# Moving the casts of a job of seven products to its head, and three position tables to a later load

## The chip, the cores and the metric

The kernel runs on one core of one Trainium2 chip. The metric is the device time of one execution in microseconds (us); the time of a version is the median of its runs. The core's engines appear under the names of the profile: PE is TensorE (matmuls; PEld are its weight loads), DVE is VectorE, ACT is ScalarE, POOL is GpSimd, SP is SyncE, which here only issues DMAs. Each engine works through its own instructions in the order in which they were recorded, and waits for the others through semaphores.

## The reference

One layer of a hybrid decoder trunk on a sequence of 512 positions and 1024 features. What matters here is the wide projection of the normed input and what is made of its columns:

```python
u = rmsnorm(x, ln1_g[i])
proj = u @ w_in[i]
q, k, v, pool_in, z, xbc, dt_raw, gate_pre = jnp.split(proj, split_idx, axis=-1)
y_a = dilated_attention_mixer(q, k, v, rel_bias) @ w_a[i]
y_b = pool_mixer(pool_in, pool_w[i], pool_scale[i]) @ w_b[i]
y_c = ssd_mixer(z, xbc, dt_raw, ...) @ w_c[i]
gates = jax.nn.sigmoid(gate_pre + b_gate[i]).reshape(b, s, N_BRANCH, D_MODEL)
merged = gates[:, :, 0] * y_a + gates[:, :, 1] * y_b + gates[:, :, 2] * y_c
x = x + merged @ w_o[i]
x = x + conv_ffn(rmsnorm(x, ln2_g[i]), ...)
return rmsnorm(x, final_g)
```

The attention has three groups of six heads with dilations 1, 4 and 16. Its scores get a bias by relative position, `rel_bias[bucket]`, which differs from group to group.

## The kernel before

Precision. Every operand of a matmul is a pair of float32r tiles, a high part and the rest. `cast` (line 185) makes the high part of a weight, `wh`, on ScalarE, in two halves; `lows` (line 208) makes the rest, `wl`, on VectorE by subtraction; `mm3` (line 228) multiplies high by high, high by low and low by high, so that `wl` is needed only in the last third of a chain of matmuls. There are three `wh` buffers, two `wl` buffers and two `raw` buffers for weights as they come from memory.

Jobs. The program is a list of jobs, one for each block of weights. The loop at line 1708 records them one after the other. For job n, `prepare` (line 1715) records first, at the head of the job: the subtraction of weight n+1, the cast of weight n+2, and the load of weight n+3. Then comes the job's body: matmuls and evacuations. `cast` is called with `spread`: its two halves are not recorded at once but put into the list `second`, and each `step()` in the body (and the `flush` loop ahead of the next job) records one of them.

Seven products. The second gate (`gate_seven(1)`), the values of attention groups 1 and 2 (`v_pair`) and the queries and keys of group 1 (`qk_sevens(1)`) are each computed by seven products of half-size blocks in place of eight. `Seven` (line 344) makes their jobs, called here by the names in the code: two, five, three, one, six, seven, and four. Five, three, six and seven have no load of their own: their weights are sums and differences that VectorE makes in the tiles W[0] and W[1] (`total`, L359, called by `then` behind a subtraction). Four's weight is loaded as raw and gets W[0] added to it, also at L359, when its cast is recorded. The order in the program is

```
gate: two five three one six seven
values: two, (gate four), five three one six seven
queries and keys: two, (values' four), five three one six seven
xbc 0, (queries' four), xbc 1, ...
```

Body of such a job (line 363): two halves of matmuls into two PSUM banks, each followed by its evacuation, and a single `step()` at the end. Two, five and three copy their banks to tiles r on ScalarE (L379). One, six and seven add the bank to r on VectorE (for the gate L741, for the values L661, for queries and keys L725); for the gate, sigmoids on ScalarE follow (L747), and `total` of the gate (L735) multiplies the merged branch by them on VectorE. One, six, seven and four accumulate in the same two banks, so a job's first matmul there waits until the sum that reads the bank is done.

What sets the order on ScalarE. Because the only step is at the end of the body, both halves of the spread cast, from the `step()` and from the `flush` loop, stand behind the job's evacuations.

Position tables. `bias_rows` (line 526) computes the biases by position, writes them to a DRAM tile `rd`, and loads six tables from there (L561): b0 to b2 for group 0, b3 to b5 for group 1, whose right half later takes group 2 (`residues`, line 572). These tables, like most working tiles, come from the pool `big`, which has 52 slots under one tag; a new tile takes a slot and waits for the last readers of the tile that held it. `rows` runs while the values of group 0 are computed; the attention of group 1 starts after the first xbc job. SP issues all loads in the order of their recording, unless a scheduler changes places between neighbours.

Of the kernel before, what the change touches and what calls it, by code (L numbers as in the profile page):

```python
# [16 lines left out]
P = 128  # L17
# [54 lines left out]
class Job:  # L72


    def __init__(self, parts, k, c, body):
        self.parts, self.k, self.c, self.body = parts, k, c, body
        self.raw = self.split = None
        self.late = self.short = False
        self.load = self.form = self.then = None


# [1 line left out]
def trunk(ctx: ExitStack, tc, out, x, rel_bias, ln1_g, w_in, b_gate, w_a, pool_w, pool_scale, w_b,  # L83
# [3 lines left out]
    act, dve, pool, pe, sp = nc.scalar, nc.vector, nc.gpsimd, nc.tensor, nc.sync  # L87
# [18 lines left out]
    def T(name, dt=F32, shape=(P, S)):  # L106
        return big.tile(list(shape), dt, name=name, tag="t")

    def MM(name):
        return psum.tile([P, S], F32, name=name, tag="mm")  # L110

    def SM(name):
        return psum.tile([P, S], F32, name=name, tag="sm")
# [230 lines left out]
    class Seven:  # L344


        def __init__(self, quarter, c, widths, product, done, name):
            R, A, B, W = {}, [], [], [None, None]

            def tile_of(i):  # L350
                W[i] = ypool.tile([P, 4, S], F32, name="w3", tag="xs")[:, :, :c]
                sp.dma_start(W[i], quarter(i, 1))

            def plus():
                for k in range(4):
                    pool.dma_start(W[0][:, k, :], quarter(0, 0)[:, k, :], accum_op=OP.add)

            def total(out, a, b, op=OP.add):
                dve.tensor_tensor(out, a, b, op)  # L359
                return out  # L360

            def job(j, raw, form, bank, use, more=False):
                def body(ws):
                    if not more:
                        bank[:] = [MM(name) for _ in range(2)]
                    for i in range(2):
                        product(bank[i], ws, side_u(j), i, more)
                        use(i, bank[i][:, :widths[i]])
                    step()
                new = Job([raw] if raw is not None else [], 4, c, body)  # L370
                new.form = form
                if raw is None:
                    new.load = lambda: None
                return new

            def keep(hi, right):
                def use(i, ps):
                    r = R[hi, right, i] = T("r7")[:, :widths[i]]
                    act.copy(r, ps)  # L379
                return use  # L380

            def end(hi, right, op=None):
                return lambda i, ps: done(hi, right, i, R.get((hi, right, i)), ps, op)

            self.two = job("A12", quarter(1, 0), None, B, keep(0, 0))
            five = job(1, None, lambda: W[0], B, keep(1, 1))
            three = job(4, None, lambda: W[1], B, keep(0, 1), True)
            one = job("A11", quarter(0, 0), None, A, end(0, 0, OP.add))
            six = job(2, None, lambda: W[0], A, end(0, 1, OP.subtract), True)
            seven = job(3, None, lambda: W[1], A, end(1, 1, OP.subtract), True)  # L390
            four = self.four = job("A22", quarter(1, 0), lambda: total(four.raw, four.raw, W[0]), A,
                                   end(1, 0), True)
            five.then = lambda: total(W[0], W[0], W[1])
            one.then = lambda: total(W[1], W[0], one.raw, OP.subtract)
            self.jobs = five, three, one, six, seven
            self.load = lambda: tile_of(0), plus, lambda: tile_of(1)
# [127 lines left out]
    bias = []  # L524

    def bias_rows():


        relb, hot = T("relb"), [T(f"hot{i}") for i in range(2)]

        hr, two = [T(f"hotr{i}", F32R) for i in range(2)], T("relp", F32R)
        rh, rl = two[:, :18], two[:, 18:36]
        dve.memset(relb[:, :18], 1.0)
        sp.dma_start(relb[:BUCKETS, :18], rel_bias)
        sp.dma_start(hot[0][:BUCKETS + 1, :S], c_hot[:, :S])
        sp.dma_start(hot[1][:BUCKETS + 1, :R_ALL - S], c_hot[:, S:])

        def part(tiles, lo, n):
            i = lo // S
            return tiles[i][:, lo - i * S:lo - i * S + n]  # L540

        def rows():
            rv = [T(f"rv{i}") for i in range(2)]
            rd = dram.tile([HEADS, R_ALL], F32, name="rdram")
            ps_r = [SM("psr0"), SM("psr1")]
            for g, (off, n) in enumerate(zip(R_OFF, R_LEN)):
                lo = off
                while lo < off + n:
                    m = min(off + n, (lo // S + 1) * S) - lo
                    for r in (rh, rl):  # L550
                        pe.matmul(part(ps_r, lo, m)[:HEADS], r[:BUCKETS + 1, 6 * g:6 * g + 6],
                                  part(hr, lo, m)[:BUCKETS + 1], start=r is rh, stop=r is rl)
                    lo += m
            for i in range(2):
                m = (S, R_ALL - S)[i]
                dve.tensor_copy(rv[i][:HEADS, :m], ps_r[i][:HEADS, :m])
                sp.dma_start(rd[:, i * S:i * S + m], rv[i][:HEADS, :m])
            for i in range(6):
                b = T(f"b{i}")
                g, width = (0, 256) if i < 3 else (1, P)  # L560
                sp.dma_start(b[:, :2 * width].rearrange("p (h c) -> p h c", h=2),  # L561
                             spans(rd, g, i % 3, P, width))
                bias.append(b)
            bias.append(rd)
            return
            yield

        def spans(rd, g, c, high, width):
            return bass.AP(tensor=rd.tensor, offset=rd.offset + R_OFF[g] + 2 * c * R_ALL,
                           ap=[[1, high], [R_ALL, 2], [1, width]])  # L570

        def residues():
            rd = bias.pop()
            for c in range(3):
                b = bias[3 + c][:, 256:]
                dve.memset(b, NEG)
                for a in range(0, P, 32):
                    sp.dma_start(b[a:a + 32].rearrange("p (h c) -> p h c", h=2)[:, :, a:a + 32],
                                 spans(rd, 2, c, 32, 32))
                yield  # L580

        def parts():
            n = BUCKETS + 1
            dve.tensor_copy(rh[:n], relb[:n, :18])
            dve.tensor_sub(rl[:n], relb[:n, :18], rh[:n].bitcast(F32))
            for i in range(2):
                m = (S, R_ALL - S)[i]
                dve.tensor_copy(hr[i][:n, :m], hot[i][:n, :m])

        return rows, parts, residues  # L590

    def bias_of(g, h):
        if g == 0:
# [890 lines left out]
    def program():  # L1484
# [11 lines left out]
        for i, job in enumerate(branch_jobs(1, w_b, YB, 8, more=range(7))):  # L1496
            if i == 1:
                yield Call(gates.load[0])
            if i == 2:
                yield Call(lambda: running.extend(after(2 * p - 4, sums_of_u(p)) for p in (2, 3)))  # L1500
                yield Call(gates.load[1])
                yield Call(gates.load[2])
            yield job
        last = None
        for group, next_ in zip(groups, groups[1:] + (None,)):
            yield group.two
# [52 lines left out]
    weights = [j for j in jobs if isinstance(j, Job)]  # L1559
# [33 lines left out]
        (b_gate[0].rearrange("(c p) -> c p", p=P), 24),  # L1593
        (pool_scale[0].rearrange("(c p) -> c p", p=P), 8)], "col")
    sp.dma_start(tri, c_tri)
    rows_of_bias, parts_of_bias, residues_of_bias = bias_rows()

    def row_squares(tb, ss, n=1, eng=dve):

# [67 lines left out]
    parts = lows(weights[1], 2)  # L1667
# [39 lines left out]
    n = 0  # L1707
    for job in jobs:
        if not isinstance(job, Job):
            job.fn()  # L1710
            continue
        while second:
            flush()
        if n >= 2:
            def prepare(n=n, later=False):

                def rest():
                    if n + 1 < len(weights):
                        low(weights[n + 1])
                    yield  # L1720
                    if n + 2 < len(weights):
                        cast(weights[n + 2], 2, spread=not later)
                    if n + 3 < len(weights):
                        fetch(weights[n + 3])
                if later:
                    return rest()
                for _ in rest():
                    pass

            if job.late:  # L1730
                job.prepare = prepare
            else:
                prepare()
            job.body(job.split)
        n += 1
# [40 lines left out]
```

## Time and profile before

| | |
|---|---|
| median of 3 runs | 1030.3 us (1029.78 to 1030.36) |
| the profiled execution, whole time | 1028.16 us |
| the profiled execution, its span | 1025.6 us |
| PE busy, share of the span | 1010.9 us, 99% |
| DVE busy | 707.7 us, 69% |
| ACT busy | 511.2 us, 50% |
| granted PE clock, mean | 0.998 |
| DMA, mean rate over the span | 119 GB/s |

Rows of the trace are read like this: a row of the timeline gives the start in us from the span's start, the duration, the engine, the line of the kernel, the operation, output<-input by the program's names, the shapes, how many instructions are merged in the row, and in brackets how long the engine was idle before and what ended that. A row of the chain of waits gives the start, the time that the chain spent there, the engine and the line. L12 is line 12 of the kernel; a line can be that of a helper, so that all casts are at L195 and nearly all matmuls at L236.

### The profile page before, as it was taken

What the parts mean: (1) busy time and instruction counts of PE and PEld (TensorE: products, weight loads), DVE (VectorE), ACT (ScalarE), POOL (GpSimd) and SP (SyncE); (2) the same over time, 40 slices, a digit from 0 to 9 for tenths busy, and PEclk for the clock granted to TensorE, in tenths of its full rate; (3) what the DMA queues carried; (4) which work ended last, traced back from release to release, by engine and by line L of the source; (5) the groups of instructions that cost most, each with busy time, mean ns of one, the idle gap of its engine ahead of it and who ended that gap; (6) DMA issues with size and microseconds to landing.
All of it is one profiled execution on the core that took longest, in us unless ns stands there. A gap on an engine that the chain in (4) does not pass through costs nothing.

```text
span 1025.6 us, 13613 instructions
## 1 busy us (share of the span) xinstructions
PE 1010.9 (99%) x5402; PEld 861.3 (84%) x5402; DVE 707.7 (69%) x886; ACT 511.2 (50%) x863; POOL 136.7 (13%) x120
## 2 busy tenths in 40 slices
PE   8999999989999999999999999999999999999997
PEld 8998877989988888888888888898888888888885
DVE  6554667568667655676889666767778768685756
ACT  5433545454536466788566234644444434433434
POOL 1781000010000000000043501102111100111002
PEclk9999999999999999999999999999999999999999
DMA  8548312044344445542254526532232232321322
GB/s 271 166 110 214 112 54 75 11 144 137 132 148 124 109 115 137 137 130 66 82 157 161 164 83 239 182 120 99 85 122 82 89 117 75 131 82 42 124 103 82
DMA packets 115629, 123.34 MB, mean 120 GB/s; under 512 B 6483, under 2 KB 96150, under 8 KB 115567
## 3 DMA queue, kind: packets, MB, share of 16 engines
q1 hardware_dynamic: 113247, 119.01, 37.3%
q0 software_dynamic: 1728, 2.62, 1.5%
q8 instruction: 42, 0.69, 0.3%
q10 hardware_dynamic: 592, 0.86, 0.3%
q14 instruction: 20, 0.16, 0.0%
HBM read 118.68 MB, written 3.00 MB: 119 GB/s over the span
## 4 chain that ended last, share of the span: by engine, by line
PE 95%; DVE 2%; ACT 2%; DMA 1%; issue 0%; ACTq 0%
PE pa L236 34%; PE pu L236 22%; PE pb L236 12%; PE pd L236 7%; PE pqk L236 6%; PE pq L236 3%; PE pa L1624 2%; PE ps L779 1%; PE pu L1414 1%; PE po L827 1%; PE ppw L236 1%; ACT wh L195 1%; DVE wl L215 1%; PE pt L813 1%; PE py L1112 1%; DMA xin<-in_x_dram 1%
## 5 line engine op out<-in xcount | busy, mean ns | idle before, releaser
L215 DVE TENSOR_TENSOR wl<-raw,wh 128x2048 fp32r<-128x2048 f32 (+3 forms) x92 | 214.1, 2328 | 60.6 <-ACT wh L195 52.7
L195 ACT CAST wh<-raw 128x1024 fp32r<-128x1024 f32 (+4 forms) x181 | 181.3, 1021 | 53.8 <-DVE raw L359 15.9
L1309 DVE SCALAR_TENSOR_TENSOR hc<-pu,fcol,hc 128x510 f32<-128x510 f32 x88 | 65.8, 748 | 56.5 <-ACT hc L1306 54.8
L236 PE MATMUL pa<-uh,wh 128*128 128x512 f32 (+1 forms) x368 | 88.9, 381 | 0.2 <-ACT wh L195 0.2
L236 PE MATMUL pa<-uh,wl 128*128 128x512 f32 (+1 forms) x368 | 86.9, 375 | 2.1 <-DVE wl L215 2.1
L236 PE MATMUL pa<-ul,wh 128*128 128x512 f32 (+1 forms) x368 | 86.8, 375 | 0.0
L236 PE MATMUL pu<-uh,wh 128*128 128x512 f32 (+1 forms) x352 | 83.5, 379 | 0.0
L236 PE MATMUL pu<-uh,wl 128*128 128x512 f32 (+1 forms) x352 | 83.5, 379 | 0.0
L236 PE MATMUL pu<-ul,wh 128*128 128x512 f32 (+1 forms) x352 | 83.5, 379 | 0.0
L236 PEld LDWEIGHTS pa<-uh,wl 128*128 128x128 f32 x368 | 66.7, 188 | 14.7 <-DVE wl L215 2.3
L236 PEld LDWEIGHTS pa<-ul,wh 128*128 128x128 f32 x368 | 66.7, 188 | 12.6
L236 PEld LDWEIGHTS pa<-uh,wh 128*128 128x128 f32 x368 | 65.3, 188 | 12.4 <-ACT wh L195 0.5
L236 PEld LDWEIGHTS pu<-uh,wl 128*128 128x128 f32 x352 | 64.2, 188 | 12.5
L236 PEld LDWEIGHTS pu<-ul,wh 128*128 128x128 f32 x352 | 64.2, 188 | 12.5
L236 PEld LDWEIGHTS pu<-uh,wh 128*128 128x128 f32 x352 | 64.1, 188 | 12.4
L1306 ACT ACTIVATE hc<-pu,fcol,fcol 128x512 f32<-128x512 f32 x40 | 31.2, 780 | 79.2 <-PE pu L236 79.2
L1314 POOL TENSOR_TENSOR hc<-hc 128x512 f32<-128x512 f32 x22 | 30.8, 1400 | 289.1 <-DVE hc L1309 244.4
L215 DVE TENSOR_TENSOR wl<-w,wh 128x2048 fp32r<-128x2048 f32 (+1 forms) x18 | 38.0, 2111 | 12.4 <-ACT wh L195 7.8
L801 ACT ACTIVATE sb<-sb,nmls 128x128 f32<-128x128 f32 (+1 forms) x72 | 30.0, 418 | 31.5 <-DVE nmls L798 21.4
L1095 POOL TENSOR_TENSOR st<-st,dts 128x512 f32<-128x512 f32 x4 | 4.2, 1053 | 228.9 <-ACT st L1103 166.8
L195 ACT CAST wh<-w 128x1024 fp32r<-128x1024 f32 (+1 forms) x36 | 32.8, 954 | 2.4 <-DVE w L341 2.4
L1311 ACT ACTIVATE hc<-hc 128x512 f32<-128x512 f32 x22 | 13.9, 632 | 39.9 <-DVE hc L1309 39.9
(409 smaller groups left out, 1923.1 us busy)
## 6 DMA issues: line engine op xcount, KB each, us to landing
raw<-in_w_in_dram SPq DMA_DIRECT2D x24, 1024.0 KB, 6.1
raw<-in_ffn_w_up_dram SPq DMA_DIRECT2D x22, 1024.0 KB, 5.2
raw<-in_w_o_dram SPq DMA_DIRECT2D x8, 1024.0 KB, 5.3
raw<-in_ffn_w_down_dram SPq DMA_DIRECT2D x8, 1024.0 KB, 5.1
raw<-in_w_in_dram SPq DMA_DIRECT2D x14, 512.0 KB, 4.8
raw<-in_w_in_dram SPq DMA_DIRECT2D x8, 768.0 KB
raw<-in_w_b_dram SPq DMA_DIRECT2D x4, 1024.0 KB, 5.2
w<-in_ffn_w_down_dram SPq DMA_DIRECT2D x4, 1024.0 KB, 5.0
```

Source lines behind the costliest of these rows:

```text
L195: (other.tensor_copy if other and i else act.copy)(job.high[:, :, o], job.raw[:, :, o])
L215: (eng or dve).tensor_tensor(l[:, :, o], job.raw[:, :, o], h[:, :, o].bitcast(F32), OP.subtract)
L236: pe.matmul(ps, l, r, start=first and n == 0, stop=last and n == total - 1, skip_group_check=onto)
L779: pe.matmul(pss[i][:, o:o + w * P], q[r, n * P:(n + 1) * P], k[r, kb * P:(kb + w) * P], start=True, stop=True)
L801: act.activation(sb[:, off:off + w * P], sb[:, off:off + w * P], AF.Exp, bias=nm[:, n, h:h + 1], accum_out=ls[:, n, h:h + 1])
L813: pe.transpose(pt[:, o:o + P], sb[:, o:o + P], eye)
L827: pe.matmul(po[DH * hh:DH * hh + DH, n * P:(n + 1) * P], V[g, kb + i][:, (2 * c + hh) * DH:(2 * c + hh + 1) * DH], probs[2 * c + hh, nb][: ...
L1306: act.activation(t, ps, AF.Identity, bias=ff["c1"][:, ff["b"] + m:ff["b"] + m + 1], scale=fw(2, m))
L1309: dve.scalar_tensor_tensor(t[:, sh:], ps[:, :S - sh], fw(k, m), t[:, sh:], OP.mult, OP.add)
L1311: act.activation(t, t, AF.Silu)
L1314: pool.tensor_tensor(a, a, t, OP.mult)
L1624: pe.matmul(first[2 * n + j][:, lo:hi], a[:, k, j * P:(j + 1) * P], b[:, k, lo:hi], start=a is wh and b is uh and k == 0, stop=a is wl and ...
```

## The change

Two things, both small in the text. Every job of seven products gets the mark `once`; while such a job is recorded, `prepare` calls `cast` without `spread`, so that both halves of the cast of weight n+2 are recorded at once, at the head of the job, ahead of its matmuls and evacuations. And the tables b3 to b5 are no longer loaded in `rows`, but by `second_table`, which `program` calls after the last `w_b` job and before the first job of the gate's group.

```diff
@@ class Job
-        self.late = self.short = False
+        self.late = self.short = self.once = False
@@ Seven.job
-                new.form = form
+                new.form, new.once = form, True
@@ bias_rows, rows
-            for i in range(6):
-                b = T(f"b{i}")
-                g, width = (0, 256) if i < 3 else (1, P)
-                sp.dma_start(b[:, :2 * width].rearrange("p (h c) -> p h c", h=2),
-                             spans(rd, g, i % 3, P, width))
-                bias.append(b)
+            table(rd, 0, 256)
             bias.append(rd)
             return
             yield
+
+        def table(rd, g, width):
+            for c in range(3):
+                b = T(f"b{c}")
+                sp.dma_start(b[:, :2 * width].rearrange("p (h c) -> p h c", h=2),
+                             spans(rd, g, c, P, width))
+                bias.append(b)
+
+        def second_table():
+            rd = bias.pop()
+            table(rd, 1, P)
+            bias.append(rd)
...
-        return rows, parts, residues
+        return rows, parts, second_table, residues
@@ program
             yield job
+        yield Call(lambda: second_table())
         last = None
@@ trunk
-    rows_of_bias, parts_of_bias, residues_of_bias = bias_rows()
+    rows_of_bias, parts_of_bias, second_table, residues_of_bias = bias_rows()
@@ the loop over jobs
-            def prepare(n=n, later=False):
+            def prepare(n=n, later=False, spread=not job.once):
...
-                        cast(weights[n + 2], 2, spread=not later)
+                        cast(weights[n + 2], 2, spread=spread and not later)
```

## The prediction

> **What bounds the kernel now.** I read the page's first two parts, then what TensorE waits for, then the stretches with waits. Columns of the page: engine, busy us, share of the span, instructions.
>
> ```profile
> span 1025.6 us, 13613 instructions
> PE 1010.9 (99%) x5402; PEld 861.3 (84%) x5402; DVE 707.7 (69%) x886; ACT 511.2 (50%) x863; POOL 136.7 (13%) x120
> ```
>
> TensorE bounds everything: no matmul is added or removed, so the change can win at most TensorE's idle time, 14.7 us, or add to it. Where is that idle time? The view of TensorE's waits, from 181 us to 310 (who waited for whom, us in total, times, longest):
>
> ```profile
> PE pa L236 <- DVE wl L215: 2.1, 1, 2.1
> PE pa L236 <- DVE r L741: 0.7, 1, 0.7
> PE pq L236 <- DVE q L725: 0.6, 1, 0.6
> ```
>
> These lie in the three groups of seven products, 181.69 to 284.60 us. Busy time there (stretch, length, PE, PEld, DVE, ACT, POOL, clock, DMA share, GB/s):
>
> ```profile
> 181.69:232.34 50.65, 47.68 (x395) 46.52 (x394) 32.15 (x24) 25.51 (x40) 3.53 (x4) 1.00 0.31 87
> 232.34:284.60 52.26, 51.47 (x362) 50.91 (x361) 39.10 (x34) 24.84 (x38) 0.00 (x0) 1.00 0.41 124
> ```
>
> TensorE is idle 2.97 us in the gate group and 0.79 us after it, at full clock, with ScalarE half busy: it is work in the wrong order, not too much work. The chain of waits (start, us, what) shows which order:
>
> ```profile
> 201.94 2.00 ACT wh L195 x2
> ...
> 207.93 0.91 ACT sg L747 x2
> 208.84 1.89 ACT wh L195 x2
> ...
> 210.76 2.29 DVE wl L215
> 213.05 0.61 DVE r L741
> ...
> 216.88 1.76 DVE wl L215
> 218.64 2.20 DVE raw L359
> 220.84 0.61 DVE r L741
> ...
> 222.29 0.90 ACT sg L747 x2
> 223.18 1.90 ACT wh L195 x2
> ...
> 225.10 2.30 DVE wl L215
> ...
> 227.45 5.05 PE pa L236 x40
> ...
> 262.25 8.64 PE pq L236 x72
> ...
> 274.46 1.16 DVE q L725 x2
> ```
>
> It is a ring. A cast (wh) of a later weight stands on ScalarE behind the sigmoids (sg) of the product that has just run; these wait for VectorE's sum (r); the sum stands behind the subtraction (wl) of the weight before; and that waits for its own cast. TensorE pays twice: it waits for a bank that a late sum still reads, and for a late wl.
>
> What it costs is best read from the starts of products:
>
> ```profile
> 207.12 0.71 PE L236 MATMUL pa<-sah,wh 128*128 128x256 f32 x4
> ...
> 213.79 0.71 PE L236 MATMUL pa<-sbh,wh 128*128 128x256 f32 x4 [0.69 <-DVE r L741]
> ...
> 219.62 0.86 PE L236 MATMUL pb<-wh,uh 128*128 128x384 f32 x4
> ...
> 224.17 0.74 PE L236 MATMUL pa<-uh,wh 128*128 128x256 f32 x4 [0.22 <-ACT wh L195]
> ...
> 232.34 0.86 PE L236 MATMUL pb<-wh,sah 128*128 128x384 f32 x4
> ...
> 236.51 0.85 PE L236 MATMUL pb<-wh,sbh 128*128 128x384 f32 x4
> ...
> 240.67 0.85 PE L236 MATMUL pb<-wh,uh 128*128 128x384 f32 x4
> ...
> 245.22 0.93 PE L236 MATMUL pb<-wh,sah 128*128 128x384 f32 x4 [0.22 <-ACT wh L195]
> ...
> 270.71 0.64 PE L236 MATMUL pq<-uh,wh 128*128 128x256 f32 x4
> ...
> 275.76 0.71 PE L236 MATMUL pq<-sah,wh 128*128 128x256 f32 x4 [0.57 <-DVE q L725]
> ```
>
> An unhindered product takes 5.83 us in the gate group (213.79 to 219.62), 4.17 with the values (232.34 to 236.51), 4.32 with queries and keys (half of 8.64, the chain's last row). Above that lie: gate six 0.84 (6.67 to seven's start), value two 0.38 (4.55), gate four 2.34 (8.17), value one 0.38 (4.55), query one 0.73 (5.05). Together 4.67 us.
>
> **The change, part one: casts at the head.** For a job of seven products, both halves of the cast of the weight two jobs on are put before its evacuations on ScalarE instead of behind them. Their count and size stay: two casts, 2.0 us for a gate weight. VectorE's and TensorE's orders are the same in both builds; only ScalarE's rows change places. I walk the queues by the durations above.
>
> Gate one (on TensorE up to 207.1): at 201.94 ScalarE now holds not six's cast, which already stands one evacuation earlier, but seven's. It ends near 203.9 instead of 210.73. Seven's subtraction (2.29) then waits only for its turn behind one's second sum (0.7 from 207.1), near 207.9, and ends at 210.2. Six's first half leaves TensorE at 207.12 + 2.9 = 210.0, its sum runs 210.2 to 210.9, and TensorE wants that bank at 212.9: 2 us of cover, and the 0.84 is gone.
>
> Gate four: after six's second sum (213.7), the subtraction for value two (1.76) ends at 215.5, and the sum for four (L359, 2.2) at 217.7. Four's cast now stands ahead of seven's sigmoids: 217.8 to 219.8, instead of from 223.18 on. Its subtraction, 2.30, ends at 222.1. TensorE reaches four at 212.9 + 5.8 + 4.2 = 222.9 and needs wl eight of its 48 matmuls later (1.0 us), at 223.9: 3.1 and 1.8 us of cover, so 0.38 and 2.34 are gone.
>
> What waits instead: ScalarE stands before four's cast from about 214.7 to 217.8, with seven's four sigmoids behind it. They end at 221.6, before 223.18 as now; only VectorE's gate multiplications read them. Nothing on TensorE does.
>
> The value and query groups go the same way: value six's subtraction waits no longer for a late cast but for value three to leave the wl buffer, at 228.7 + 2 x 4.17 = 237.0, and ends at 238.8; one's first sum follows as soon as TensorE gives it, near 239, and the 0.38 is gone. Query six: two sums of 1.16 us after one's first half end just as one's second half does, so of 0.73 I take 0.6 and leave 0.1. The heads whose cast waits for a sum on VectorE (value's and query's four) hold up only evacuations with over 2 us to spare.
>
> The casts' other two needs hold by the same walk. The wh buffer (three of them) is that of the job before, which TensorE has just left. The raw weight of gate four is asked for here:
>
> ```profile
> 202.77 0.39 SPq L182 DMA_DIRECT2D raw<-in_w_in_dram  x1
> raw<-in_w_in_dram SPq DMA_DIRECT2D x24, 1024.0 KB, 6.1
> ```
>
> It lands at 208.9 and is first read by the sum at 215.5. Part one: 0.84 + 0.38 + 2.34 + 0.38 + 0.6 = 4.5 us.
>
> [...] By busy time alone part one would be 2.97 + 0.79 = 3.8 us; by starts it is 4.5, and the starts carry the sum, since each wait also shows a drained pipe as busy.
>
> **Part two: three tables later.** The three 128 KB tables of groups 1 and 2 leave the queue of SP near 72 us and enter it behind value two's raw weight; in the changed build the latest thing they wait for is a matmul in the second half of the last job before the groups, near 180.
>
> ```profile
> 176.12 5.48 PE pa L236 x24
> ...
> 71.77 3.21 SPq L561 DMA_DIRECT2D b<-rdram  x6
> 180.00:190.00 10.00, 10.00 (x94) 9.34 (x93) 4.71 (x4) 3.69 (x7) 0.00 (x0) 1.00 0.00 0
> 308.53 0.68 DVE L794 SCALAR_TENSOR_TENSOR sb<-ps,b 128x512 f32<-128x512 f32 x1
> ```
>
> Six tables issue in 3.2 us, so three in 1.6; the DMA engines are idle from 180 to 190, and SP is free until 202.77. First use is at 308.53. Cost nothing, with over 20 us of cover in front of the weights.
>
> But the tables take no slots of the shared pool meanwhile, so every tile after them lands in another slot, and waits for other old readers. In the two builds' waits I find one that matters:
>
> ```profile
> 166.50 0.59 ACT L1018 ACTIVATE east<-pact 16x512 f32<-16x512 f32 x1 [3.23 <-PE po L827]
> ...
> 167.50 0.87 PE L827 MATMUL po<-sb,v 128*64 128x128 f32 x10 [0.82 <-ACT sb L814]
> ```
>
> Before, `east` stands in a slot that the po matmuls read: ScalarE waits 3.23 us, the copy of sb behind it is late, and TensorE waits 0.82 us. In the changed build `east` waits for no matmul. It can run at 163.3 (166.50 less 3.23), and the copy ends one us later, as now; TensorE asks for it at 166.7 (167.50 less 0.82), 2 us after. That is 0.8 us more. The other changed waits point at releases long past. Bounds: zero, if another wait takes its place, to 1.0 with the drain; I take 0.8, by the wait's own row.
>
> **Sum.** 4.5 + 0.8 = 5.3 us. After 284.60 TensorE waits for almost nothing until the tail, and loads are released by the same subtractions, so I let it reach the end. The profiled execution took 1028.16 us, 2.1 below the median of 1030.3; it would become 1022.9. Against the median: 1030.3 - 5.3 = 1025.0 us. About 2.1 us (0.2%) is what a measurement can tell from no change.
>
> **Rivals.** Gate four still waits (12%). If the serial run from 213.7 to 222.1 (subtraction, sum, cast, subtraction) is 4 us later than walked, the cover of 1.8 is used up and four keeps its 2.3: 5.3 - 2.3 = 3.0 us won, 1027.3. For it: this run is the longest on VectorE, and the cast now stands in its midst. Against: all its durations are measured ones.
>
> The change does not do what it says (8%). If a cast at the head cannot start before the old place, because wh or raw is not free, then only the slot's 0.8 is left, or later loads swallow the rest: 1029.5, within 0.2%. For it: three wh buffers only. Against: the walk above finds each free on time; the raw loads land with 6 us in hand.
>
> Slower (6%): the tables block SP. If their slots came free only when gate results do, near 232, four's raw weight behind them would be asked for at 232 instead of 202.77, land at 238, and TensorE would stand from 222.9 until cast and subtraction are through (238 + 2.2 + 2.0 + 2.3 = 244.5) less 1: some 20 us, 1030.3 - 5.3 + 20 = 1045. From 211 on (223.9 less 2.3, 2.0, 2.2 and 6.1) every us of delay costs one, and past 216 the change loses. The named releases, near 180, speak against it.
>
> **How the numbers follow.** Forecast 74%, its own range 1024.0 to 1026.5: busy time and slot alone give 3.8 + 0.8 = 4.6 (1025.7), all starts with the drain 4.67 + 1.0 = 5.7 (1024.6), and half a us for the median itself. To hold 8 in 10 I reach up into the first rival: 1023.7 to 1027.8. Faster 74 + 12 = 86%; same 8%; slower 6%.
>
> **What would show it.** In the changed profile: no wait of pa for wl or r, of pq for q, of po for sb; each gate product's start 5.8 us after the last; four's cast straight behind L359, sigmoids after it; value five near 228 on the old clock; the tables issued near 180. Any new wait of a matmul for wh, or for a raw load behind the tables, makes it wrong.

## The result, and the profile after

| | before | after |
|---|---|---|
| median of 6 runs each | 1030.03 us (1028.81 to 1030.36) | 1021.44 us (1021.24 to 1021.96) |
| the profiled execution, whole time | 1028.16 us | 1021.86 us |
| its span | 1025.6 us | 1019.9 us |

The ratio is 0.992, with a 95% interval of 0.9907 to 0.9933. The change gains 8.6 us by these medians, where the prediction had 5.3: the direction is right, the size too small, and the time lies below the predicted range. First what the profile shows of the steps.

The head of the page after, and then all that TensorE waits for in the whole span (who waited for whom, us in total, times, longest):

```profile
span 1019.9 us, 13619 instructions
...
PE 1010.3 (99%) x5402; PEld 862.2 (85%) x5402; DVE 707.4 (69%) x886; ACT 511.3 (50%) x863; POOL 136.4 (13%) x120
```

```profile
PE uT L1649 <- DVE diag L1661: 1.7, 2, 1.3
PE pa L1591 <- DVE ones L1582: 1.1, 1, 1.1
```

Busy times are those of before, engine by engine. The waits for wl, r and q in the groups of seven are gone, and so is the wait for sb at the po matmuls. What is left lies at the start of the kernel. TensorE's busy time moved by 0.6 us, the span by 5.7: nothing was made cheaper, TensorE only stands less.

The same two stretches as before (stretch, length, PE, PEld, DVE, ACT, POOL, clock, DMA share, GB/s):

```profile
181.69:232.34 50.65, 50.65 (x416) 50.32 (x415) 36.78 (x30) 29.32 (x47) 3.53 (x4) 1.00 0.36 100
232.34:284.60 52.26, 52.26 (x361) 51.09 (x360) 37.77 (x32) 22.09 (x34) 0.00 (x0) 1.00 0.43 134
```

TensorE now works through both without a gap, 416 matmuls in the first where there were 395.

The starts of the products, from the timeline of TensorE:

```profile
206.33 0.64 PE L236 MATMUL pa<-sah,wh 128*128 128x256 f32 x4
...
212.09 0.64 PE L236 MATMUL pa<-sbh,wh 128*128 128x256 f32 x4
...
217.85 0.86 PE L236 MATMUL pb<-wh,uh 128*128 128x384 f32 x4
...
222.01 0.64 PE L236 MATMUL pa<-uh,wh 128*128 128x256 f32 x4
...
227.76 0.86 PE L236 MATMUL pb<-wh,sah 128*128 128x384 f32 x4
...
236.09 0.85 PE L236 MATMUL pb<-wh,uh 128*128 128x384 f32 x4
...
240.25 0.85 PE L236 MATMUL pb<-wh,sah 128*128 128x384 f32 x4
...
265.67 0.64 PE L236 MATMUL pq<-uh,wh 128*128 128x256 f32 x4
...
270.06 0.71 PE L236 MATMUL pq<-sah,wh 128*128 128x256 f32 x4
...
278.90 2.00 PE L236 MATMUL pa<-uh,wh 128*128 128x512 f32 x8
```

Every gate product takes 5.75 or 5.76 us, every value product 4.16 or 4.17. Product by product against before:

| product | before | after | gained | predicted |
|---|---|---|---|---|
| gate six | 6.67 | 5.76 | 0.91 | 0.84 |
| value two | 4.55 | 4.16 | 0.39 | 0.38 |
| gate four | 8.17 | 5.75 | 2.42 | 2.34 |
| value one | 4.55 | 4.16 | 0.39 | 0.38 |
| query one | 5.05 | 4.39 | 0.66 | 0.6 |

From gate six's start to the first matmul behind the groups it took 284.60 - 207.12 = 77.5 us, and now takes 278.90 - 206.33 = 72.6: 4.9 us. Behind the groups nothing of it is lost again: 741.0 us are left to the end of the span in both.

The queue order that the walk predicted around gate four, on ScalarE and then on VectorE (start, us, engine, line, operation):

```profile
213.01 0.91 ACT L754 ACTIVATE sg<-r,col 128x256 f32<-128x256 f32 x2 [1.97 <-DVE r L748]
216.96 2.00 ACT L195 CAST wh<-raw 128x1024 fp32r<-128x1024 f32 x2 [3.04 <-DVE raw L359]
218.87 1.70 ACT L754 ACTIVATE sg<-r,col 128x256 f32<-128x256 f32 x4
```

```profile
214.56 2.29 DVE L359 TENSOR_TENSOR raw<-raw,w 128x2048 f32<-128x2048 f32 x1
...
218.99 2.29 DVE L215 TENSOR_TENSOR wl<-raw,wh 128x2048 fp32r<-128x2048 f32 x1 [0.25 <-ACT wh L195]
```

Four's cast waits 3.04 us for its sum, with seven's four sigmoids behind it, as walked; the subtraction ends at 221.28. TensorE reaches gate four at 222.01 and wants wl a us later: 1.7 us of cover, where the prediction had 1.8. The price that ScalarE pays, 3 us of standing, costs TensorE nothing.

The tables and `east` (the queue of SP; ScalarE):

```profile
177.61 1.77 SPq L566 DMA_DIRECT2D b<-rdram  x3
```

```profile
163.74 0.58 ACT L1025 ACTIVATE east<-pact 16x512 f32<-16x512 f32 x1
```

The three tables issue near 178 in 1.77 us; `east` waits for nothing. What that is worth is read from the chain of waits, before and after: a row at the start of the kernel, then the first row of the po matmuls and the next row of pa.

```profile
21.32 1.75 PE uT L1690 x16
...
165.45 1.07 PE po L827 x16
...
169.81 2.77 PE pa L236 x12
```

```profile
21.88 1.75 PE uT L1698 x16
...
166.00 1.68 PE po L834 x28
...
169.13 2.77 PE pa L236 x12
```

From po to pa it took 169.81 - 165.45 = 4.36 us and now takes 169.13 - 166.00 = 3.13: 1.23 us, where the prediction had 0.8 and at most 1.0. The first rows show something else: the profiled execution after was 0.56 us late by 21 us, ahead of both parts of the change. Over all the profiles of the experiments below, that row of uT starts between 21.1 and 22.2 us, and one of the late ones (21.86) belongs to a kernel with the tables at their old place; so the spans of single executions scatter by about a us, whatever the change does.

### The profile page after: what moved, and what is told of

It is laid out like the page before. It is cut to its first block, busy times and chain, and to the rows that moved or that the text cites. A ratio compares the mean times of both kernels' runs of the same rounds, so it can differ in the third digit from the quotient of the medians.

```text
span 1019.9 us, 13619 instructions
## 1 busy us (share of the span) xinstructions
PE 1010.3 (99%) x5402; PEld 862.2 (85%) x5402; DVE 707.4 (69%) x886; ACT 511.3 (50%) x863; POOL 136.4 (13%) x120
## 4 chain that ended last, share of the span: by engine, by line
PE 98%; DMA 1%; DVE 0%; ACT 0%; ACTq 0%; issue 0%
PE pa L236 36%; PE pu L236 22%; PE pb L236 12%; PE pd L236 7%; PE pqk L236 6%; PE pq L236 3%; PE pa L1632 2%; PE ps L786 1%; PE pu L1421 1%; PE ppw L236 1%; PE po L834 1%; PE pt L820 1%; PE py L1119 1%; DMA xin<-in_x_dram 1%; PE pyo L1126 1%; PE pst L1107 0%
```

## The experiments

Every kernel was timed beside the kernel before. Medians of before in the three comparisons: 1029.23 (21 runs), 1029.47 (15) and 1029.55 (18), so below the 1030.3 of the first three runs and the 1030.03 of the first six.

**The halves alone, and both ends again.** In the first kernel only the hunk of the casts stands, in the second only that of the tables; the others are before and after, unchanged.

```diff
@@ casts_only, against before
-                new.form = form
+                new.form, new.once = form, True
...
-            def prepare(n=n, later=False):
+            def prepare(n=n, later=False, spread=not job.once):
...
-                        cast(weights[n + 2], 2, spread=not later)
+                        cast(weights[n + 2], 2, spread=spread and not later)
@@ tables_only, against before
+            table(rd, 0, 256)
...
+        yield Call(lambda: second_table())
```

> The casts at the head of a job of seven products, the six tables loaded where they were. Theory A (each part acts alone; the 2 us between the profiled execution of before and its median are stalls that this execution happened not to have): the ring costs the usual execution more than the profiled one, so the casts win 6.5 to 7.5 us, and TensorE still waits 0.8 us for the copy of sb near 167. Theory B (the time over the sum comes from the tables, as less load on the queue of SP near 72 us): the casts win 4.5 to 5 us only. The trace should show the products of the seven in a row in both.

> The second three tables loaded with the second gate, the casts spread as before. Theory A: 0.8 to 1.3 us faster, no wait of TensorE near 167, the ring's waits (2.1, 0.7, 0.6) unchanged. Theory B: 3 to 4 us faster, with something shortened between 60 and 110 us.

> The kernel before, unchanged. If the profiled execution of before was a quick one of its kind, this one has a span nearer to 1028 us and waits of TensorE for wl, r, q and sb that sum to 2 us more than the 4.5 us shown there, or waits at a place that had none. If the difference lies outside the span, its span is 1025.6 again and the time around the span is over 4 us.

> The changed kernel, unchanged. Without the ring there is little left that could vary: a span within 0.7 us of 1019.9, and no wait of TensorE beyond its start in any execution.

| kernel | median, us | ratio to before, 95% interval | executions at clock 0.998 or 0.999: number, spans | at 0.997 or less: number, spans |
|---|---|---|---|---|
| before, beside these | 1029.23 | | 8: 1025.3 to 1026.1 | 13: 1026.7 to 1027.8 |
| before_again | 1029.41 | 0.9999 (0.999 to 1.0008) | 3: 1025.4 to 1025.5 | 8: 1026.8 to 1027.7 |
| tables_only | 1027.58 | 0.9986 (0.9977 to 0.9995) | 2: 1024.6 to 1024.8 | 9: 1025.7 to 1026.7 |
| casts_only | 1022.76 | 0.9939 (0.9926 to 0.9951) | 5: 1020.5 to 1021.0 | none |
| after_again | 1021.78 | 0.9928 (0.9915 to 0.994) | 5: 1019.1 to 1019.9 | none |

Two things follow. The halves add up: among executions at the high clock the casts are worth 1025.6 - 1020.6 = 5.0 us (medians of the spans), the tables 1025.6 - 1024.7 = 0.9, both 1025.6 - 1019.7 = 5.9. By the medians over all executions it is 6.5 for the casts, at the lower edge of theory A, and 1.65 for the tables, above A's 1.3 and far from B's 3 to 4. (Of the 1.65, 0.6 us lie outside the span: 1.86 us in tables_only against 2.47 before.) The places where the two work do not touch: casts_only still has the wait of 0.8 us for sb, tables_only still has the ring's 2.1, 0.7 and 0.6.

And the kernels that keep the ring fall into two groups, 1.1 to 1.6 us apart and told apart by the granted clock; those without it do not. Theory A looked for stalls that the profiled execution did not have; the repeat of the kernel before, profiled at 1025.5 us, has the same waits and cannot show any, because both profiled executions of that kernel had the high clock. That of tables_only had the low one, and shows where it is lost. Its wait at gate four, and the product behind it in the chain of waits:

```profile
PE pa L236 <- DVE wl L215: 2.1, 1, 2.1
```

```profile
225.96 6.53 PE pa L236 x40
```

The wait is the same 2.1 us as before, but the 40 matmuls that took 5.05 us (227.45 in the chain of before) take 6.53. In steps of 1 us, the clock is the number ahead of the last two; tables_only, then before:

```profile
225.00:226.00 1.00, 0.04 (x1) 0.04 (x1) 1.00 (x2) 0.79 (x2) 1.00 (x3) 1.00 0.00 0
226.00:227.00 1.00, 1.00 (x8) 1.00 (x9) 1.00 (x2) 0.00 (x0) 1.00 (x2) 1.00 0.60 49
227.00:228.00 1.00, 1.00 (x8) 1.00 (x7) 1.00 (x3) 0.00 (x0) 0.48 (x1) 0.62 0.94 167
228.00:229.00 1.00, 1.00 (x7) 1.00 (x7) 1.00 (x2) 0.23 (x1) 0.05 (x1) 0.50 0.99 286
229.00:230.00 1.00, 1.00 (x6) 1.00 (x6) 0.98 (x1) 0.61 (x2) 0.84 (x1) 0.50 0.95 283
230.00:231.00 1.00, 1.00 (x8) 1.00 (x7) 0.99 (x1) 0.00 (x0) 0.00 (x0) 0.67 1.09 255
231.00:232.00 1.00, 1.00 (x11) 1.00 (x10) 0.77 (x1) 0.00 (x0) 0.00 (x0) 1.00 1.18 209
```

```profile
228.00:229.00 1.00, 1.00 (x11) 1.00 (x10) 1.00 (x2) 0.00 (x0) 0.48 (x1) 1.00 0.93 149
```

About a us after TensorE has begun again, the clock is halved, and TensorE gets 6 to 8 matmuls through in a us instead of 11, all the time "busy". That gave a new theory: the wait at gate four costs twice, once its own length, and in most executions another 1.5 us through the clock. The rival is that the clock falls for some other reason and only seems to follow the ring.

**The wait kept, TensorE kept busy in it.** Dummy matmuls fill the wait; the ring stays.

```diff
@@ filler, against before: ahead of gate four's first wl matmul
+    filler = []
...
+                if filler and n == 8:
+                    ps_f = SM("fill")
+                    for _ in range(filler.pop()):
+                        pe.matmul(ps_f[:, :256], ones, uh[:, 0, :256], start=True, stop=True)
...
+                    if name == "pa" and j == "A22":
+                        filler.append(16)
```

> The kernel before, with 16 dummy matmuls of 128x256 put into gate four just ahead of its first wl matmul, where TensorE waits 2.06 us; they write a bank that nobody reads. Clock theory (the wait itself costs 2 us, and in most executions the granted clock is halved behind it, which costs another 1.4): the ring stays as late as before, but TensorE is no longer idle, so the span is that of the quick executions of the kernel before, 1025.6, in every execution; all granted clocks 0.998; median 1027.9 to 1028.2 against 1029.3. Rival (the lower clock comes from something else, such as the chip or the execution's phase): two groups of spans stay, about two in three at 0.996 to 0.997, and the median is 1029.3. Third: the dummies are not hidden and cost up to 1.9 us: 1031.

```profile
224.68 0.73 PE L238 MATMUL pa<-uh,wh 128*128 128x256 f32 x4 [0.22 <-ACT wh L195]
225.25 0.64 PE L238 MATMUL pa<-ul,wh 128*128 128x256 f32 x4
225.72 2.03 PE L244 MATMUL fill<-uh,ones 128*128 128x256 f32 x16
227.95 0.74 PE L238 MATMUL pa<-uh,wl 128*128 128x256 f32 x4 [0.20 <-DVE wl L215]
```

This timeline shows gate four's products as late as before, with the dummies in the gap and a wait of 0.2 us left. All 11 executions have a clock of 0.998 or 0.999 and spans of 1025.7 to 1026.6; beside them the kernel before had 11 of 15 at 0.997 or less, 1026.8 to 1028.5. The median is 1028.41 against 1029.47; the ratio, 0.9995 (0.9986 to 1.0004), cannot tell so little by itself, the clocks can. (The median is 0.2 above what I expected; the four quick executions beside it have spans of 1025.5 to 1026.1.) Work that computes nothing makes the kernel no slower and takes the group at the low clock away: the clock falls because of the wait.

**Waits put into the changed kernel.** Gate four's subtraction is repeated on VectorE, so that a wait of a chosen length comes back without the ring.

```diff
@@ after_stall, against after; stall_short has (c, c // 4), stall_long (c, c, c // 4)
+            def again():
+                h, l = four.split
+                for w in (c, c * 3 // 4):
+                    dve.tensor_tensor(l[:, :, :w], four.raw[:, :, :w], h[:, :, :w].bitcast(F32),
+                                      OP.subtract)
+            if name == "pa":
+                four.then = again
```

> The changed kernel, with gate four's subtraction on VectorE repeated for 1.75 of its length (+4.0 us), which uses up the 1.8 us of cover that the prediction gave it. By that cover: a wait of about 2.2 us comes back for wl at gate four, and only there. Clock theory: executions fall into two groups again, one at +2.2 us over the changed kernel (span about 1022) with a clock of 0.998 and a larger one at +3.6 (1023.4) with 0.996 to 0.997; median near 1025.2. Rival (a stall costs its own length only): one group, span 1022, median 1023.9. If the cover is larger than 4.0 us: 1021.7, nothing.

> The changed kernel, with gate four's subtraction on VectorE repeated for 1.25 of its length (+2.9 us). The run with +4.0 us left TensorE waiting 2.3 us, so the cover is 1.7 us and a wait of 1.2 us comes back. If the clock reacts to a wait of that length: two groups of spans, +1.2 and +2.6 over the changed kernel's 1019.7, clocks of 0.997 among them, median above 1023.5. If it does not: one group, span near 1020.9, all clocks 0.998 to 0.999, median 1022.9.

> The same with 2.25 of its length (+5.2 us): a wait of 3.5 us. If the clock falls by the wait's phase, more of the executions fall for a longer wait: nearly all at a clock of 0.996 to 0.997, span 1019.7 + 3.5 + 1.5 = 1024.7, median 1026.7. If it doesn't depend on length: two groups again, 1023.2 and 1024.6, about one in three at 0.998. Rival (a stall costs its own length): one group at 1023.2, median 1025.2.

What TensorE waits for at gate four, in stall_short, after_stall and stall_long:

```profile
PE pa L236 <- DVE wl L400: 1.3, 1, 1.3
```

```profile
PE pa L236 <- DVE wl L400: 2.3, 1, 2.3
```

```profile
PE pa L236 <- DVE wl L400: 3.6, 1, 3.6
```

| kernel | wait, us | median, us | ratio to before | at 0.998 or more: number, spans | at 0.997 or less |
|---|---|---|---|---|---|
| stall_short | 1.3 | 1023.27 | 0.9939 (0.9926 to 0.9952) | 6: 1020.9 to 1021.8 | none |
| after_stall | 2.3 | 1025.48 | 0.9963 (0.9951 to 0.9976) | 2: 1022.3 to 1022.5 | 3: 1023.3 to 1023.7 |
| stall_long | 3.6 | 1028.05 | 0.9984 (0.9976 to 0.9993) | none | 12: 1024.4 to 1026.0 |

4.0 us more of subtraction left 2.3 us of waiting, so the cover was 1.7, as read above. A wait of 1.3 us never cost the clock in six executions, one of 2.3 in three of five, one of 3.6 in all twelve: two groups came back in a kernel without the ring. (The spans of stall_short scatter by 0.9 us, up to 1021.8 where I expected 1020.9, but all at the high clock; the profiled one of 1021.8 was among the late starters, 22.2 us in the row of uT.) For the long wait I expected 1026.7 and got 1028.05: by its own length the span would be 1019.7 + 3.6 = 1023.3, and it is 1.1 to 1.6 above that in five executions, 2.3 to 2.7 in seven. The profile is one of the five; in it the clock falls once more behind the wait:

```profile
226.00:227.00 1.00, 0.92 (x7) 0.92 (x8) 1.00 (x3) 0.00 (x0) 0.67 (x1) 1.00 1.02 169
227.00:228.00 1.00, 1.00 (x7) 1.00 (x6) 1.00 (x3) 0.00 (x0) 0.00 (x0) 0.54 0.90 106
228.00:229.00 1.00, 1.00 (x7) 1.00 (x6) 1.00 (x2) 0.00 (x0) 0.00 (x0) 0.50 0.74 215
229.00:230.00 1.00, 1.00 (x7) 1.00 (x7) 1.00 (x1) 0.84 (x2) 0.00 (x0) 0.50 1.05 272
230.00:231.00 1.00, 1.00 (x8) 1.00 (x8) 0.97 (x2) 0.00 (x0) 0.00 (x0) 0.76 1.10 303
231.00:232.00 1.00, 1.00 (x11) 1.00 (x10) 0.90 (x1) 0.00 (x0) 0.00 (x0) 1.00 0.38 118
```

The mean clock is 0.997 in all five and 0.996 in all seven, which fits a low clock that lasted longer or came again in the seven; no profile here shows it.

**The casts by group.** The mark only for the gate group, and only for values and queries.

```diff
@@ gate_only; rest_only has name != "pa"
-                new.form, new.once = form, True
+                new.form, new.once = form, name == "pa"
```

> The changed kernel, with the cast at the head for the gate group only; values and queries keep it in the last step. By the starts: what was won at value two and gate four depends on the gate group's order (0.84 + 2.34 + 0.38, with the clock's 1.4), what is given back is value one 0.38 and query one 0.6: median 1021.7 + 1.0 = 1022.7, all clocks 0.998. Rival (the rings are one: a late cast in the value group delays the gates too): gate waits return, 1026 or more.

> The changed kernel with the cast at the head for values and queries only; the gate group casts in its last step, as before. By the starts: value one's 0.38 and query one's 0.6 are won, with the slot's 1.2; gate six's 0.84 and gate four's 2.3 stay, with the clock behind it: wait of pa for wl about 2.1 us, two groups of spans, about 1023.3 and 1024.7, median 1026.8. Rival (the late casts of the value group cause gate four's wait): no wait for wl, 1022 to 1023.

TensorE's waits in the groups, gate_only and then rest_only:

```profile
PE pq L236 <- DVE q L732: 0.6, 1, 0.6
PE pb L236 <- ACT wh L195: 0.2, 1, 0.2
```

```profile
PE pa L236 <- DVE wl L215: 2.1, 1, 2.1
PE pa L236 <- DVE r L748: 0.7, 1, 0.7
PE pa L236 <- ACT wh L195: 0.2, 1, 0.2
```

Each group has its own ring. gate_only has 1022.5 us, ratio 0.9938 (0.9926 to 0.9951), all five clocks at 0.998 or more. rest_only has 1026.9, ratio 0.9968 (0.9956 to 0.9981), with three executions at 1023.5 to 1023.9 and four at 0.997 with 1025.0 to 1025.3: 1026.8 was expected.

**The slot or the move of the tables.** Two tries to give every tile its old slot back while the tables stay late.

```diff
@@ slots_held, against after: at the tables' old place
+            for c in range(3):
+                dve.memset(T(f"held{c}")[:, :1], 0.0)
@@ slots_kept: these three are kept in the list held, and written again where the tables are loaded
+            for t in held:
+                dve.memset(t[:, :1], 0.0)
```

> The changed kernel, with three slots of the pool taken at the old place of the tables by tiny memsets, so that every later tile stands in the slot that it had before; the tables are still loaded late. Theory (the gain of the second part is the slot of east, not the move of the tables): ScalarE's wait for po matmuls and TensorE's 0.8 us wait for sb come back, median 1022.7 (the casts alone gave 1022.76). Rival (the tables' move itself): 1021.7, no wait for sb.

> The changed kernel again with three slots taken at the tables' old place, now held until the tables are loaded (a second tiny memset there), so that east stands in the slot that the po matmuls read, as before; the tables are still loaded late. Theory (the second part's gain is the slot of east): ScalarE's wait of 3.2 us for po and TensorE's of 0.8 us for sb come back, span 1020.5 to 1020.9, median 1022.7 as with the casts alone. Rival (the late loads give the gain): no wait for sb, 1021.7.

The first missed its aim: with no later use the three slots came free again at once, `east` kept the slot that it has in the changed kernel, and the run repeats that kernel (1021.62 us, ratio 0.9929, 0.9917 to 0.9942). In the second `east` stands where it stood before. What ScalarE waits for from 155 to 175 us, and TensorE in the span:

```profile
ACT east L1032 <- PE po L841: 3.2, 1, 3.2
```

```profile
PE po L841 <- ACT sb L828: 0.8, 1, 0.8
```

Both waits are back; from po to pa it takes 4.36 us again (165.63 to 169.99 in the chain of waits), against 3.13 in slots_held (166.33 to 169.46). The gain of the second part is gone: 1022.75 us, ratio 0.9936 (0.9921 to 0.9951), against 1022.76 of the casts alone. Five of its six spans are 1020.5 to 1020.9, 1.1 us above slots_held by the medians; the sixth, 1022.0, has a clock of 0.996. So a low clock can come without a wait of 2 us, but it did in this one alone of 49 executions of the kernels that have none (after and its repeat, casts_only, gate_only, slots_held, slots_kept, stall_short, filler).

## Why the prediction was right in its mechanism and wrong in its size

*Part one, 4.5 us.* Right, and a little small: 4.9 by the starts, 5.0 by the casts alone. Each of the five products gave its term, all within 0.1 us, together 4.77. The other 0.14 came from products that I had called unhindered: gate seven took 5.83 us and now takes 5.76. The walk through the queues holds, with a cover of 1.7 for 1.8, which the run with 4.0 us of extra subtraction confirms from the other side. Adding up starts was right too, as two rows of TensorE before show:

```profile
212.47 0.64 PE L236 MATMUL pa<-sah,wl 128*128 128x256 f32 x4
213.79 0.71 PE L236 MATMUL pa<-sbh,wh 128*128 128x256 f32 x4 [0.69 <-DVE r L741]
```

Rows of this shape start 0.48 us apart where nothing waits, but each is shown for 0.64. So gate seven's start came 0.84 us late, of which 0.69 are shown as idle, and counted in this way each of the five waits costs 0.15 to 0.17 us more than its idle time. What the prediction calls a drained pipe is this much that the rows show as busy.

*Part two, 0.8 us.* The cause is right, shown by slots_kept: the slot gives the gain, the later loads nothing. The term was too small, and so was its upper bound of 1.0: I took it from the wait's own row, but TensorE lost 1.23 us between po and pa. The medians give 0.9 to 1.1, with the scatter of the start in them.

*The sum against the profiled execution.* I had 1028.16 - 5.3 = 1022.9, and it became 1021.86. The spans differ by 5.7: 4.9 in the groups, 1.2 at po and 0.1 between, less 0.56 for the late start of the execution after. The time outside the span fell as well, from 2.56 us to 1.96. That is not one execution's doing: the median is 2.47 in the 54 later executions of the kernel before and 2.06 in the five of after_again. I had put this term at nothing; no profile shows what it is.

*The sum against the median.* This is the step that failed: "The profiled execution took 1028.16 us, 2.1 below the median of 1030.3; it would become 1022.9. Against the median: 1030.3 - 5.3 = 1025.0 us." It took the 2.1 us as something that the change leaves alone. But 1.5 of them belong to the ring. In the three later comparisons the kernel before ran 20 times at the high clock, with a median span of 1025.65, and 34 times at the lower one, with 1027.2. The profile had caught one of the quick kind, so every row that I read showed a clock of 1.00, and I wrote that TensorE stood idle "at full clock". The median lies among the 34 each time (for the six runs of the first comparison no clock is on record), and the change removes the wait behind which the clock falls. So the gain against the median is 5.9 + 1.5 = 7.4 us by the spans, and the repeated pair measured 1029.23 - 1021.78 = 7.5. That these agree so well is in part luck: the 0.4 us outside the span comes on top, and the median of before, 1029.23, lies 0.3 below that of its slow executions alone, 1029.55. What the first comparison's 8.6 has beyond that lies in its six runs of before, 0.5 to 0.8 us above the later medians, and its six of after, 0.3 below the repeat; its interval, 6.9 to 9.6 us (0.67% to 0.93% of 1030), holds both. Why that first level was higher stays open. The range failed with it: its lower end had half a us for the median.

*The rivals.* None came in. Gate four no longer waits, the change does what it says, and SP was not held up. What I lacked was a rival on the good side: that the same wait costs more in the executions that were not profiled. The page held a hint: 2.1 us, 0.2%, between the profiled execution and the median, while the three runs agreed within 0.6.

## What to carry to other kernels

When the profiled execution is quicker than the median, the difference is part of the kernel: ask which wait could cost more in the other executions, and look at the granted clock and span of each of them before the gain is carried over to the median. A wait of 2 us on TensorE cost more than its length in two executions of three here, one of 1.3 us in none of six; filling the wait with dummy matmuls showed that the clock was involved (no low clock in 11 executions, where the kernel before had 11 in 15), without touching what causes the wait. When a change moves allocations in a rotating pool, read the waits of tiles that it does not name: here 1.2 us of TensorE's time came from one tile in another slot. And the time that a wait costs is read from the start of one piece of work to the start of the next, here 1.23 us where the wait's own row had 0.82.

## What the runs showed of the hardware that was not expected

TensorE's clock was halved for about 3.4 us behind a wait of 2.1 us and behind one of 3.6, in the two profiles that caught it. The length is an estimate from the rows of 1 us, with the clock taken as either full or half in the rows that lie between 1.00 and 0.50. In tables_only a granted 0.62 in the first us then means half clock for 0.76 of it, 0.67 in the last for 0.66: 0.76 + 1 + 1 + 0.66 = 3.4 us at half clock. The long wait gives the same: 0.92 + 1 + 1 + 0.48 = 3.4. It begins about a us after the matmuls are back, at 227.24 in the first (back at 225.96), at 227.08 in the second (back at 226.08). With the ring's wait of 2.1 us, a mean clock of 0.997 or less came in 55 of 83 executions (before 34 of 54, before_again 8 of 11, tables_only 9 of 11, rest_only 4 of 7); a wait of 1.3 us brought it in none of six, one of 2.3 in three of five, one of 3.6 in all twelve. What decides it in a single execution, no run shows. That 3.4 us is always the length is not shown either: the seven executions of stall_long at 0.996 lost a us more, and single ones of the kernel before at 0.994 and 0.995 had spans up to 1030.3, with no profile of them.
